# First weights loaded between the parts of the memory and used channel by channel; GpSimd adds up squares and layer-norm sums

## Chip, cores and metric

One NeuronCore of a Trainium2 chip runs the whole program; nothing is shared with another core. The metric is the device time of one execution in microseconds (us). The kernel before was timed three times. Engines are named as the profile names them: PE (TensorE matmuls), PEld (its weight loads), DVE (VectorE), ACT (ScalarE), POOL (GpSimd), SP (SyncE, which only issues DMAs).

## The reference

Two residual blocks over 256 tokens of width 1024, all in float32. Only the first block's opening and its convolution branch are touched by the change:

```python
h     = rms_norm(x, norm_g);  mem_h = rms_norm(mem, mem_norm_g)      # sums over 1024 channels
c_glu, c_gate, d_q, d_k, d_v, d_gate, x_q, x_gate, merge = split(h @ w_in)
k, v  = split(mem_h @ w_mem_kv)                                      # memory's keys and values
u     = conv31(a * sigmoid(b)) + dw_b                                # depthwise, causal, a, b = split(c_glu)
u     = layer_norm(u, ln_g, ln_b)                                    # needs sum(u) and sum(u*u) over channels
y_conv = (silu(u) * silu(c_gate)) @ w_conv_proj
y     = g0 * y_conv + g1 * y_diff + g2 * y_mem;  x = x + y @ w_out
```

The second block (stick-breaking attention, a recurrence, and a retrieval of 128 of 16384 single-neuron experts for each token) follows and ends the program.

## The kernel before

Activations lie transposed: 128 partitions, 8 chunks of channels, 256 tokens. Weights of the first block and of the second block's projections come as 94 blocks of 1 MB (`STREAM`, in the order of use), each as two halves `raw` of 128x1024 elements, issued by SP. A float32 product is made of three fast ones: `prep` (line 234) has ACT round a half to `whi` (line 247) and DVE subtract to get the rest, `wlo` (line 248); an activation is split in the same way into a high and a low part. A block is then 48 matmuls of 128x256, three for each of 16 pairs of chunk and column (`linT`, line 292, for transposed results, `linN`, line 330, for results with tokens on the partitions). `raw` has 5 buffers, `whi` and `wlo` 4 each, so that a cast waits until PE has used the half that lies four halves back. Matmuls against `ONES` (the statistics, named `stat` or `att`) are in full float32.

Start of the program (lines 475 to 505): the memory `m_t` is loaded in four pieces of two chunks, then the two halves of the first weights, then `x` in two pieces, constants, and then the stream. ACT and DVE multiply the memory by its gain and split it (`gain_col`, line 410: `mgh`, `mgl`); ACT squares it and PE sums the squares over partitions and chunks in eight `ONES` matmuls (`rms_sq`, line 435); `rstd_of` makes the reciprocal root on ACT and DVE, `tok_scalar` turns it to tokens on partitions (PE, line 420). The first four blocks, `linN`, multiply the memory; the scale is applied when ACT evicts the result to `vm` (line 503). Beside them `x` is normalised (`rms_cols`, lines 428 and 405: for each chunk DVE makes `nrm`, ACT casts it to `hh`, DVE subtracts to `hl`); block 5 is the first that needs `hh` and `hl`.

The convolution (lines 523 to 549) is 248 operations `tap` on DVE, 128x256 each, 62 for each pair of chunks. They go into a list `bg` and are taken from it in portions (`BG`, by an estimated cost) after each block; `background(.., True)` pins them behind the last `wlo`. They run beside all of the branches up to line 689. Then lines 693 to 699 make the two sums of the layer norm: ACT squares `cacc`, and PE adds `cacc` and the squares over partitions and chunks, 16 `ONES` matmuls. Each is issued as soon as its data is there in the scheduler's own reckoning, so they are spread over the last 60 us of the taps. Lines 700 to 717 make the normalised `cn`, lines 719 to 720 gate it.

A scheduler places every instruction on its engine's queue when the program is built; on the chip each queue runs strictly in that order. POOL does almost nothing until the second block's retrieval, at 600 us.

## Time and profile before

| | |
|---|---|
| three runs | 1292.05, 1288.19, 1291.80 us; median 1291.8 us |
| the profiled execution | 1291.35 us, of which the span of instructions 1289.6 us |
| PE busy | 1253.5 us (97%) |
| DVE busy | 937.0 us (73%) |
| ACT busy | 457.3 us (35%) |
| POOL busy | 214.6 us (17%), 1.5 us of it before 620 us |
| DMA | 340.76 MB, mean 264 GB/s |
| chain that ended last | PE 43%, issue 20%, DMA 16%, DVE 11%, POOL 6%, ACT 3% |

Busy time of PE is modelled from overlapping matmuls, so a full row does not say that PE ran at its peak; the distance between the starts of two matmuls says more. Waits are read from the profile's list of who waited for whom, order and distances from the timeline, and the chain shows what ended last. The granted clock of PE was at its upper level (2.4 GHz) in all of the first 600 us.

### The profile page before, as it was taken

Reading aid. Unit: us, or ns where it says so; the run is one execution under the profiler, and the core shown is the slowest. Engines: PE = TensorE matmul, PEld = TensorE weight load, DVE = VectorE, ACT = ScalarE, POOL = GpSimd, SP = SyncE. Lnnn points to the kernel's source line nnn. Section 1 sums busy time; section 2 is a strip of 40 time slices with the busy share of each in tenths; the row PEclk is TensorE's granted clock in tenths of the full one; section 3 lists DMA queues with packets and bytes.
Section 4 is the critical chain, followed back from the end, with each engine's and each line's share of the span. In section 5 each row is a group of like instructions: output and inputs, shape, how many; then the busy total and the mean of one; then the engine's idle time right before and its main releaser. Section 6 shows DMA issues by size and latency. Waiting matters only on the chain.

```text
span 1289.6 us, 24478 instructions
## 1 busy us (share of the span) xinstructions
PE 1253.5 (97%) x9948; PEld 1211.0 (94%) x9948; DVE 937.0 (73%) x1806; ACT 457.3 (35%) x741; POOL 214.6 (17%) x222
## 2 busy tenths in 40 slices
PE   8999999999999999998999899999999999999995
PEld 7999999989999999977999899999999999999884
DVE  6889988888998777855899864588545886445444
ACT  7545677578646556955431100010000000000001
POOL 0000000000000000000013443222342225333331
PEclk9999999999999999999999999999999999999998
DMA  8655443434565664423577999999999999999996
GB/s 294 189 194 182 164 138 124 132 116 147 164 200 161 196 202 157 148 67 99 181 235 240 354 409 409 409 408 363 382 383 342 356 360 392 409 409 408 409 409 231
DMA packets 94865, 340.76 MB, mean 264 GB/s; under 512 B 10576, under 2 KB 12048, under 8 KB 94624
## 3 DMA queue, kind: packets, MB, share of 16 engines
q1 hardware_dynamic: 66752, 237.98, 52.0%
q0 software_dynamic: 28000, 101.22, 20.4%
q8 instruction: 78, 1.28, 0.4%
q14 instruction: 35, 0.29, 0.1%
HBM read 338.01 MB, written 1.05 MB: 263 GB/s over the span
## 4 chain that ended last, share of the span: by engine, by line
PE 43%; issue 20%; DMA 16%; DVE 11%; POOL 6%; ACT 3%; POOLq 0%; SPq 0%; DVEq 0%; ACTq 0%
DMA gat<-in_vrow,gi 10%; PE lin L308 10%; PE lin L307 10%; PE lin L309 10%; POOL gat L1186 6%; DMA gat<-in_urow,gi 5%; DVE acc L1211 2%; PE lin L341 1%; DVE gat L1193 1%; PE lin L343 1%; PE lin L342 1%; DVE wlo L248 1%; PE stat L459 1%; ACT whi L247 1%; DVE I L983 1%
## 5 line engine op out<-in xcount | busy, mean ns | idle before, releaser
L1177 PE MATMUL y<-ga,w 128*128 128x160 f32 x2048 | 293.0, 302 | 5.6 <-DMA w<-in_v 2.8
L1177 PEld LDWEIGHTS y<-ga,w 128*128 128x128 f32 x2048 | 279.9, 190 | 13.3 <-DMA w<-in_v 10.4
L288 PE MATMUL lin<-h3f,w 128*128 128x160 f32 x2048 | 290.5, 302 | 1.7 <-ACT ga L1166 1.7
L288 PEld LDWEIGHTS lin<-h3f,w 128*128 128x128 f32 x2048 | 281.5, 191 | 2.3 <-ACT ga L1166 1.9
L248 DVE TENSOR_TENSOR wlo<-raw,whi 128x1024 fp32r<-128x1024 f32 x188 | 229.1, 1221 | 64.2 <-ACT whi L247 63.5
L247 ACT CAST whi<-raw 128x1024 fp32r<-128x1024 f32 x188 | 196.2, 1049 | 167.2 <-PE lin L308 123.8
L308 PE MATMUL lin<-hl,whi 128*128 128x256 f32 x704 | 200.2, 284 | 0.0
L309 PE MATMUL lin<-hh,wlo 128*128 128x256 f32 x704 | 199.8, 284 | 0.0
L307 PE MATMUL lin<-hh,whi 128*128 128x256 f32 x704 | 199.8, 284 | 0.0
L1211 DVE SCALAR_TENSOR_TENSOR acc<-gat,cG,acc 128x1024 f32<-128x1024 f32 x94 | 120.7, 1284 | 95.3 <-DMA gat<-in_vrow,gi 49.2
L1193 DVE CUSTOM_DVE_ANT_0 gat<-gat,hrow 128x1024 f32<-128x1024 f32 x96 | 116.6, 1224 | 29.8 <-DMA gat<-in_urow,gi 16.2
L1186 POOL DMA_INDIRECT gat<-in_urow,gi x96 | 103.4, 1077 | 198.9 <-DVE sG L1193 188.9
L309 PEld LDWEIGHTS lin<-hh,wlo 128*128 128x128 f32 x704 | 132.6, 188 | 2.2 <-issue 1.9
L308 PEld LDWEIGHTS lin<-hl,whi 128*128 128x128 f32 x704 | 132.6, 188 | 1.7 <-issue 1.4
L307 PEld LDWEIGHTS lin<-hh,whi 128*128 128x128 f32 x704 | 132.5, 188 | 1.4 <-issue 1.0
L1186 POOL DMA_INDIRECT gat<-in_vrow,gi x96 | 93.3, 972 | 162.6 <-DVE acc L1211 127.4
L1166 ACT ACTIVATE ga<-lin 128x320 f32<-128x320 f32 x64 | 27.9, 437 | 249.8 <-PE lin L288 216.7
L535 DVE SCALAR_TENSOR_TENSOR cacc<-ub,VT,cacc 128x256 f32<-128x256 f32 x240 | 103.7, 478 | 0.0
L955 POOL DMA_DIRECT2D fold<-in_con x1 | 0.7, 703 | 596.9 <-DVE gate L924 596.9
L1292 ACT COPY ga<-y 128x160 f32<-128x160 f32 x4 | 1.2, 292 | 236.2 <-PE y L1177 236.2
L1155 DVE SCALAR_TENSOR_TENSOR ga<-gp,ga 128x256 f32<-128x256 f32 (+1 forms) x60 | 29.1, 510 | 74.6 <-PE gp L1144 55.3
L308 PE MATMUL lin<-h3lo,whi 128*128 128x256 f32 x128 | 37.3, 291 | 2.3 <-DVE h3lo L384 2.3
(373 smaller groups left out, 2099.9 us busy)
## 6 DMA issues: line engine op xcount, KB each, us to landing
raw<-in_wcat SPq DMA_DIRECT2D x188, 512.0 KB
w<-in_u SPq DMA_DIRECT2D x128, 512.0 KB
w<-in_v SPq DMA_DIRECT2D x128, 512.0 KB
gat<-in_urow,gi POOLq DMA_INDIRECT x96
gat<-in_vrow,gi POOLq DMA_INDIRECT x96
m_t<-in_memT SPq DMA_DIRECT2D x4, 256.0 KB
xr<-in_xT SPq DMA_DIRECT2D x2, 512.0 KB
kT<-in_keysT SPq DMA_DIRECT2D x1, 1024.0 KB
```

Of the source, the lines that this page charges most:

```text
L247: nc.scalar.copy(h, raw)
L248: state["sub"] = nc.vector.tensor_sub(l, raw, h.bitcast(F32))
L288: nc.tensor.matmul(ps[:, a], ws[a][:, c * P:(c + 1) * P], x[:, c], start=c == 0, stop=c == 7)
L307: nc.tensor.matmul(ps[:, a], wh, ah[:, c], start=(a, c) in first, stop=False)
L308: nc.tensor.matmul(ps[:, a], wh, al[:, c], start=False, stop=False)
L309: nc.tensor.matmul(ps[:, a], wl, ah[:, c], start=False, stop=(a, c) in last)
L535: nc.vector.scalar_tensor_tensor(cacc[:, c], s, w, cacc[:, c], op0=ALU.mult, op1=ALU.add)
L1155: state["dve"] = nc.vector.scalar_tensor_tensor(g_[:, :, tl], p_, 1.0 / GSCALE, g_[:, :, tl], op0=ALU.mult, op1=ALU.mult)
L1177: nc.tensor.matmul(yT[c // 2][:, c % 2, :D], ws[a][:, c * P:(c + 1) * P], g[:, a], start=False, stop=i == 63 and (a, c % 2) == (1, 1))
L1186: nc.gpsimd.indirect_dma_start(g, None, src, bass.IndirectOffsetOnAxis(gi[:, 0, k:k + 1].bitcast(U32), 0))
L1193: nc.vector.tensor_tensor_reduce(out=g, in0=g, in1=h, scale=1.0, scalar=0.0, op0=ALU.mult, op1=ALU.add, accum_out=sG[:, k:k + 1])
L1211: state["sum"] = nc.vector.scalar_tensor_tensor(acc[m], g, cG[:, k:k + 1], acc[m], op0=ALU.mult, op1=ALU.add)
```

## The change

1. The first weights come between the pieces of the memory: `m_t` piece 1, the vectors, half 1 of block 1, pieces 2 and 3, half 2, piece 4. The halves of block 2 are issued before `x` and the constants.
2. Gains and weight splits are written in the order in which those loads come, and block 1 (`linN(.., True)`) goes channel by channel, both token halves of a chunk one after the other, so that it can begin with the first chunks. The third product of each triple is now the one with `wlo`.
3. The memory's squares are made by POOL (four `tensor_mul` of 128x512); POOL adds the last three up (two `tensor_add`). PE sums two matmuls' worth ahead of block 1 and two behind it, four in place of eight.
4. The layer norm's sums: after each pair of chunks ACT squares `cacc`, and POOL (for the first three pairs) or DVE (for the last) adds it to a running sum: `rx` for the values, `sums[0]` for the squares. PE then needs 3 `ONES` matmuls in place of 16.
5. Four small operations for the second block's recurrence (`la`) are held back until the last merge gate.

```diff
-        def prep(i):
+        def load(i, a):
+            raw = spool.tile([P, 1024], F32, name="raw", bufs=5)
+            nc.sync.dma_start(raw, srcs[i][:, a * 1024:(a + 1) * 1024])
+            return raw
+
+        def prep(i, raws=None, between=None):
...
-                raw = spool.tile([P, 1024], F32, name="raw", bufs=5)
-                nc.sync.dma_start(raw, srcs[i][:, a * 1024:(a + 1) * 1024])
+                raw = load(i, a) if raws is None else raws[a]
+                if between is not None:
+                    between(a)
...
-        def linN(act):
+        def linN(act, channelwise=False):
...
+            if channelwise:
+                seq = [(t, c) for c in range(8) for t in range(2)]
+                first, last = seq[:1], seq[-1:]
+            else:
+                seq = [(t, c) for t in range(2) for c in range(8)]
+                first, last = [(0, 0), (1, 0)], [(0, 7), (1, 7)]
...
+                nc.tensor.matmul(ps[:, t], xh, wh, start=(t, c) in first, stop=False)
+                nc.tensor.matmul(ps[:, t], xl, wh, start=False, stop=False)
+                nc.tensor.matmul(ps[:, t], xh, wl, start=False, stop=(t, c) in last)
...
-            nc.sync.dma_start(m_t[:, 0:2], memT[:, 0:2])
+            def m_load(k):
+                nc.sync.dma_start(m_t[:, 2 * k:2 * k + 2], memT[:, 2 * k:2 * k + 2])
+
+            m_load(0)
             nc.sync.dma_start(VT, vec)
-            for k in range(1, 4):
-                nc.sync.dma_start(m_t[:, 2 * k:2 * k + 2], memT[:, 2 * k:2 * k + 2])
-            prep(0)
+            raws = [load(0, 0)]
+            m_load(1)
+            m_load(2)
+            raws.append(load(0, 1))
+            m_load(3)
+            raws1 = [load(1, a) for a in range(2)]
...
+            m_gains(0)
+            prep(0, raws, lambda a: [gain_col(m_t, "mem_norm_g", mgh, mgl, c) for c in (2, 3, 4, 5)] if a else None)
+            for c in (6, 7):
+                gain_col(m_t, "mem_norm_g", mgh, mgl, c)
+
+            stm = statp()
+            msq = [smt("sqs", 512, 1), smt("sq"), smt("sq")]
+            for k in range(4):
+                q = msq[min(k, 2)] if k < 3 else smt("gate", 512, 3)
+                nc.gpsimd.tensor_mul(q.rearrange("p (a b) -> p a b", a=2), m_t[:, 2 * k:2 * k + 2],
+                                     m_t[:, 2 * k:2 * k + 2])
+                if k > 1:
+                    nc.gpsimd.tensor_add(msq[1], msq[1], q)
+                if k == 0:
+                    for b in range(2):
+                        nc.tensor.matmul(stm[:, :T], ONES, q[:, b * T:(b + 1) * T], start=b == 0, stop=False)
+            rm = smt("rm", T, 1)
+            prep(1, raws1)
...
             for j in range(4):
-                ps = linN((mgh, mgl))
+                ps = linN((mgh, mgl), j == 0)
+                if j == 0:
+                    for b in range(2):
+                        nc.tensor.matmul(stm[:, :T], ONES, msq[1][:, b * T:(b + 1) * T], start=False, stop=b == 1)
+                    rstd_of(stm[:, :T], 1.0 / 1024, T, out=rm)
+                    rmt = tok_scalar(rm, "rmt")
...
+            def conv_sums(j):
+
+                def f():
+                    e = nc.gpsimd if j < 3 else nc.vector
+                    x = cacc[:, 2 * j:2 * j + 2]
+                    sq = smt("sq" if j else "sqs", 512, 2 if j else 1)
+                    nc.scalar.square(sq.rearrange("p (a b) -> p a b", a=2), x)
+                    if j == 0:
+                        sums.append(sq)
+                        e.tensor_add(rx, x[:, 0], x[:, 1])
+                    else:
+                        for k in range(2):
+                            e.tensor_add(rx, rx, x[:, k])
+                        e.tensor_add(sums[0], sums[0], sq)
+                return f
...
+                bg.append((0.0, conv_sums(j)))
                 background(BG[0], True)
...
-            for c in range(0, NC, 2):
-                sq = smt("sq")
-                nc.scalar.square(sq.rearrange("p (a b) -> p a b", a=2), cacc[:, c:c + 2])
-                for k in range(2):
-                    nc.tensor.matmul(s1[:, :T], ONES, cacc[:, c + k], start=c + k == 0, stop=c + k == 7)
-                    nc.tensor.matmul(s2[:, :T], ONES, sq[:, k * T:(k + 1) * T], start=c + k == 0, stop=c + k == 7)
+            nc.tensor.matmul(s1[:, :T], ONES, rx, start=True, stop=True)
+            for k in range(2):
+                nc.tensor.matmul(s2[:, :T], ONES, sums[0][:, k * T:(k + 1) * T], start=k == 0, stop=k == 1)
...
-            nc.scalar.activation(la, lam, AF.Abs)
+            with tc.issue_after(state["gate"].ins):
+                nc.scalar.activation(la, lam, AF.Abs)
```

What the change moves on the queues is shown at three places. The numbers ahead of the rows are places in an engine's queue; lines in the changed kernel are its own.

PE between block 1 and block 2 of the changed kernel (L352 to L354 are `linN`'s three products; before, L341 to L343 with all eight `stat` matmuls in the first rows of the queue), and POOL from the start:

```order
47 L352 MATMUL lin<-whi,mgh 128x256
48 L353 MATMUL lin<-whi,mgl 128x256
49 L354 MATMUL lin<-wlo,mgh 128x256
50 L537 MATMUL stat<-sq,ONES 128x256 x2
51 L352 MATMUL lin<-whi,mgh 128x256
```

```order
6 L520 ISA
7 L520 TENSOR_TENSOR sqs<-m_t 128x512
8 L520 TENSOR_TENSOR sq<-m_t 128x512 x2
9 L523 TENSOR_TENSOR sq<-sq 128x512
10 L520 TENSOR_TENSOR gate<-m_t 128x512
11 L523 TENSOR_TENSOR sq<-sq,gate 128x512
12 L587 TENSOR_TENSOR rx<-cacc 128x256
13 L590 TENSOR_TENSOR rx<-rx,cacc 128x256 x2
14 L591 TENSOR_TENSOR sqs<-sqs,sq 128x512
```

Block 2 stands on PE behind the two matmuls of L537, and these wait for POOL's sixth operation (row 11). The two of the first squares (L526) are the head of the queue. ACT where `x` is normalised, before and then with the change (`hh` is line 384 before and 395 now, the cast of weights 247 and 253, the eviction `vm` 503 and 541):

```order
31 L247 CAST whi<-raw 128x1024
32 L384 CAST hh<-nrm 128x256 x2
33 L247 CAST whi<-raw 128x1024
34 L384 CAST hh<-nrm 128x256 x2
35 L503 ACTIVATE vm<-lin,rmt 128x256 x2
36 L247 CAST whi<-raw 128x1024
37 L384 CAST hh<-nrm 128x256 x2
38 L247 CAST whi<-raw 128x1024
39 L384 CAST hh<-nrm 128x256 x2
```

```order
25 L395 CAST hh<-nrm 128x256 x2
26 L253 CAST whi<-raw 128x1024
27 L395 CAST hh<-nrm 128x256
28 L253 CAST whi<-raw 128x1024
29 L541 ACTIVATE vm<-lin,rmt 128x256 x2
30 L557 ACTIVATE le<-stat 128x2
31 L395 CAST hh<-nrm 128x256 x5
```

Five of the eight casts now stand behind the twelfth weight cast (row 28) and the eviction of block 4. The third place is PE in the layer norm's sums: before, ten of the 16 matmuls in one piece, and now all three that are left, 482 linear matmuls later:

```order
2461 L308 MATMUL lin<-hl,whi 128x256
2462 L698 MATMUL stat<-cacc,ONES 128x256
2463 L699 MATMUL att<-sq,ONES 128x256
2464 L698 MATMUL stat<-cacc,ONES 128x256
2465 L699 MATMUL att<-sq,ONES 128x256
2466 L698 MATMUL stat<-cacc,ONES 128x256
```

```order
2939 L314 MATMUL lin<-hl,whi 128x256
2940 L751 MATMUL stat<-rx,ONES 128x256
2941 L315 MATMUL lin<-hh,wlo 128x256
2942 L313 MATMUL lin<-hh,whi 128x256
2943 L314 MATMUL lin<-hl,whi 128x256
2944 L753 MATMUL att<-sqs,ONES 128x256 x2
```

The last four of the 16 stood up to linear matmul 2812 of the program; the three now stand at 2855 to 2858.

## Rows read from the trace of the kernel before

**Rows 1.** Time by stage: busy us of each engine, granted clock, DMA share, GB/s.
```profile
core 0: us, PE busy (x) PEld busy (x) DVE busy (x) ACT busy (x) POOL busy (x), PEclk, DMA share, GB/s
...
11.00:21.00 10.00, 10.00 (x71) 9.44 (x70) 7.94 (x12) 8.21 (x15) 0.00 (x0) 1.00 1.01 397
...
250.00:420.00 170.00, 169.26 (x1366) 163.38 (x1365) 149.64 (x268) 113.77 (x182) 0.00 (x0) 1.00 0.50 157
```

**Rows 2.** Chain that ended last, in order of time: start us, us, what.
```profile
401.13 0.43 PE stat L698 x2
402.15 0.86 PE att L699 x4
```

**Rows 3.** Timeline of the start, all engines, PE's rows: start us, us, what.
```profile
18.50 0.28 PE L341 MATMUL lin<-whi,mgh 128*128 128x256 f32 x1
...
18.62 0.28 PE L342 MATMUL lin<-wlo,mgh 128*128 128x256 f32 x1
...
18.95 0.60 PE L420 MATMUL stat<-ONES,rm 1*128 1x1 f32 x4
```

**Rows 4.** Chain that ended last: block 5 begins.
```profile
37.98 0.22 PE lin L307
```

**Rows 5.** Timeline of ACT at the start: memory's fourth piece, second weight cast, casts of x.
```profile
8.36 0.91 ACT L412 ACTIVATE mgh<-m_t,VT 128x256 fp32r<-128x256 f32 x2 [0.49 <-DMA m_t<-in_memT]
...
11.26 1.03 ACT L247 CAST whi<-raw 128x1024 fp32r<-128x1024 f32 x1
...
37.46 0.71 ACT L384 CAST hh<-nrm 128x256 fp32r<-128x256 f32 x2
```

**Rows 6.** Timeline of DVE at the start: splits of memory, weights and x.
```profile
7.50 0.88 DVE L413 SCALAR_TENSOR_TENSOR mgl<-m_t,VT,mgh 128x256 fp32r<-128x256 f32 x2 [0.53 <-ACT mgh L412]
...
10.85 1.23 DVE L248 TENSOR_TENSOR wlo<-raw,whi 128x1024 fp32r<-128x1024 f32 x1 [0.50 <-ACT whi L247]
...
38.74 0.75 DVE L384 TENSOR_TENSOR hl<-nrm,hh 128x256 fp32r<-128x256 f32 x2
```

**Rows 7.** Timeline of POOL in the second block: products of 128x256.
```profile
626.87 1.53 POOL L998 TENSOR_TENSOR cs<-V 128x256 f32<-128x256 f32 x1 [25.58 <-DVE V L988]
636.47 0.62 POOL L998 TENSOR_TENSOR cs<-V 128x256 f32<-128x256 f32 x1 [8.08 <-DVE V L988]
...
719.09 0.62 POOL L998 TENSOR_TENSOR cs<-V 128x256 f32<-128x256 f32 x1 [1.56 <-DVE V L988]
```

**Rows 8.** Timeline of DVE around 627 us.
```profile
626.70 1.22 DVE L248 TENSOR_TENSOR wlo<-raw,whi 128x1024 fp32r<-128x1024 f32 x1
...
628.43 0.43 DVE L982 MAX8 BS<-cs 128x8 f32<-128x256 f32 x1 [0.24 <-POOL cs L998]
```

**Rows 9.** Timeline of DVE around 719 us.
```profile
719.25 1.53 DVE L1193 CUSTOM_DVE_ANT_0 gat<-gat,hrow 128x1024 f32<-128x1024 f32 x1
```

**Rows 10.** The page's costliest groups: count | busy us, mean ns of one | idle before.
```profile
L1193 DVE CUSTOM_DVE_ANT_0 gat<-gat,hrow 128x1024 f32<-128x1024 f32 x96 | 116.6, 1224 | 29.8 <-DMA gat<-in_urow,gi 16.2
```

**Rows 11.** Timeline of PE: first and last of ten statistics matmuls before the layer norm.
```profile
344.30 0.59 PE L698 MATMUL stat<-cacc,ONES 128*128 128x256 f32 x2
...
348.43 0.47 PE L309 MATMUL lin<-hh,wlo 128*128 128x256 f32 x1
```

**Rows 12.** Ten-microsecond windows before the layer norm (columns as in rows 1).
```profile
350.00:360.00 10.00, 10.00 (x88) 10.00 (x87) 9.80 (x19) 5.22 (x6) 0.00 (x0) 1.00 0.46 144
...
400.00:410.00 10.00, 10.00 (x82) 9.84 (x81) 6.25 (x12) 6.64 (x10) 0.00 (x0) 1.00 0.48 157
```

**Rows 13.** Timeline of DVE: last tap and the layer norm's mean.
```profile
397.32 0.48 DVE L535 SCALAR_TENSOR_TENSOR cacc<-ub,VT,cacc 128x256 f32<-128x256 f32 x1
...
401.60 0.42 DVE L701 TENSOR_SCALAR rm<-stat 128x256 f32<-128x256 f32 x1 [1.38 <-PE stat L698]
```

**Rows 14.** Timeline of ACT around the layer norm: squares or weight casts, their waits.
```profile
391.40 1.05 ACT L247 CAST whi<-raw 128x1024 fp32r<-128x1024 f32 x1 [1.76 <-PE lin L308]
...
392.97 1.28 ACT L354 ACT_TABLE_LOAD   x1
```

More of the change, by code (lines that the diff above doesn't have):

```diff
@@ L334, in linN @@
             ps = lin_ps[0].tile([P, 2, T], F32, name="lin")
-            for t in range(2):
-                for c in range(8):
-                    wh = hs[c // 4].rearrange("p (c j) -> p c j", c=4)[:, c % 4]
-                    wl = ls[c // 4].rearrange("p (c j) -> p c j", c=4)[:, c % 4]
-                    xh = ah[:, c, t * P:(t + 1) * P]
-                    xl = al[:, c, t * P:(t + 1) * P]
-                    nc.tensor.matmul(ps[:, t], xh, wh, start=c == 0, stop=False)
-                    nc.tensor.matmul(ps[:, t], xh, wl, start=False, stop=False)
-                    nc.tensor.matmul(ps[:, t], xl, wh, start=False, stop=c == 7)
+            if channelwise:
[4 more added lines that the diff above has]
+                first, last = [(0, 0), (1, 0)], [(0, 7), (1, 7)]
+            for t, c in seq:
+                wh = hs[c // 4].rearrange("p (c j) -> p c j", c=4)[:, c % 4]
+                wl = ls[c // 4].rearrange("p (c j) -> p c j", c=4)[:, c % 4]
+                xh = ah[:, c, t * P:(t + 1) * P]
+                xl = al[:, c, t * P:(t + 1) * P]
+                nc.tensor.matmul(ps[:, t], xh, wh, start=(t, c) in first, stop=False)
+                nc.tensor.matmul(ps[:, t], xl, wh, start=False, stop=False)
+                nc.tensor.matmul(ps[:, t], xh, wl, start=False, stop=(t, c) in last)
             ahead()
@@ L479, in build, with m_gains @@
             m_t = bigt("m_t")
-            nc.sync.dma_start(m_t[:, 0:2], memT[:, 0:2])
+            def m_load(k):
+                nc.sync.dma_start(m_t[:, 2 * k:2 * k + 2], memT[:, 2 * k:2 * k + 2])
+            m_load(0)
             nc.sync.dma_start(VT, vec)
-            for k in range(1, 4):
-                nc.sync.dma_start(m_t[:, 2 * k:2 * k + 2], memT[:, 2 * k:2 * k + 2])
-            prep(0)
+            raws = [load(0, 0)]
[4 more added lines that the diff above has]
+            raws1 = [load(1, a) for a in range(2)]
             for k in range(2):
                 nc.sync.dma_start(x_t[:, 4 * k:4 * k + 4], xT[:, 4 * k:4 * k + 4])
+            mgh, mgl = bigt("mgh", F32R), bigt("mgl", F32R)
+            def m_gains(a):
+                for c in range(4 * a, 4 * a + 2):
+                    gain_col(m_t, "mem_norm_g", mgh, mgl, c)
+            m_gains(0)
+            prep(0, raws, lambda a: [gain_col(m_t, "mem_norm_g", mgh, mgl, c) for c in (2, 3, 4, 5)] if a else None)
+            for c in (6, 7):
+                gain_col(m_t, "mem_norm_g", mgh, mgl, c)
+            stm = statp()
[11 more added lines that the diff above has]
+            prep(1, raws1)
             nc.sync.dma_start(CT, con)
             nc.sync.dma_start(ident, con0[:, :P])
-            mgh, mgl = bigt("mgh", F32R), bigt("mgl", F32R)
-            for c in range(NC):
-                gain_col(m_t, "mem_norm_g", mgh, mgl, c)
-            rm = smt("rm", T, 1)
-            stm = statp()
-            for c in range(0, NC, 2):
-                rms_sq(m_t, stm, c, NC)
-            rstd_of(stm[:, :T], 1.0 / 1024, T, out=rm)
-            rmt = tok_scalar(rm, "rmt")
             vm = big.tile([P, 2, 1024], F32, name="vm", tag="big")
@@ L536, in tap @@
                 return f
+            sums = []
+            def conv_sums(j):
[12 more added lines that the diff above has]
+                return f
             for j in range(4):
@@ L693, in build @@
             s1, s2 = statp(), attp()
-            for c in range(0, NC, 2):
-                sq = smt("sq")
-                nc.scalar.square(sq.rearrange("p (a b) -> p a b", a=2), cacc[:, c:c + 2])
-                for k in range(2):
-                    nc.tensor.matmul(s1[:, :T], ONES, cacc[:, c + k], start=c + k == 0, stop=c + k == 7)
-                    nc.tensor.matmul(s2[:, :T], ONES, sq[:, k * T:(k + 1) * T], start=c + k == 0, stop=c + k == 7)
+            nc.tensor.matmul(s1[:, :T], ONES, rx, start=True, stop=True)
+            for k in range(2):
+                nc.tensor.matmul(s2[:, :T], ONES, sums[0][:, k * T:(k + 1) * T], start=k == 0, stop=k == 1)
             mu, mm, var = smt("rm", T, 1), smt("nrm", T), smt("nrm", T)
```

## The prediction

> **What bounds the kernel now.** I read the stages by time first. From 11 to 21 us PE is busy all the time and the DMA engines are full, at 397 GB/s; from 250 to 420 us PE is busy for 169.26 of 170 us, DVE for 149.64 and ACT for 113.77 [rows 1]. PE is what time is made of here, so a PE instruction that goes is worth its whole length, as long as DVE still delivers the split weights in time. The chain gives the length of the instructions in question: one full-float32 matmul of 128x256 takes 0.43 us (two take 0.86) [rows 2], while the products of a block start 0.12 us apart [rows 3], 48 x 0.12 = 5.8 us for a block. The timelines of the start then give the marks: block 1 is over and the scale's transposition begins at 18.95 us [rows 3], block 5, the first that needs `x` normalised, begins at 37.98 us [rows 4]. Between the two lie three blocks and two small groups of statistics, 19.03 us, which the change keeps in content.
>
> **The start of the program.** The change takes four of eight statistics matmuls off PE, 4 x 0.43 = 1.7 us, and lets block 1 begin with the first chunks. What it needs does not come earlier: before, the second half of the first weights was the last of 2.28 MB, and ACT cast it at 11.26 us without a wait; now the memory's fourth piece is the last of the same 2.28 MB. The memory's second piece now ends 1.23 MB, as its fourth did before, for which ACT waited until 8.36 us [rows 5]; I take 8.1 us for POOL. Were DVE left alone, the second half's `wlo` would be done at some 12.6 us, 22 products would follow it, and block 1 would end at 15.4 us; with two matmuls of statistics (0.86) block 2 would begin at 16.3 us.
>
> But DVE is not left alone. POOL's operation at 626.87 us took 1.53 us where one alone takes 0.62 [rows 7]: it was issued 0.17 us after a `wlo` on DVE that ended at 627.92, and ended 0.48 us behind that [rows 8]. The other way round, POOL's operation of 719.09 us ran to 719.71 [rows 7], and the DVE operation issued at 719.25 took 1.53 us [rows 9] against a mean of 1.224 [rows 10]. In both cases DVE had two inputs in SBUF and POOL read SBUF, and the later one stood until the earlier was through. That is what the splits `mgl` (memory and `mgh`) and `wlo` (`raw` and `whi`) are, and what POOL's six new operations are.
>
> The Trainium skill (SBUF — State Buffer, section Who interferes with whom) has it as a rule that such a pair excludes each other for the whole instruction and that the order of issue decides who waits. By that rule, with which these rows agree in both directions, the start comes out late as in the next paragraph; without it, early as in the first rival.
>
> So I add up both engines' work on one resource, from 8.1 us until block 2 can begin. POOL has five operations of 512 elements left. Their length is not in the trace: between 0.62 us (no more than for 256) and 1.24 us (twice that); I take 1.2, since the work is by element: 6.0 us. DVE has three `wlo` at 1.2 us and six `mgl` at 0.44 us [rows 6], 6.2 us. That is 12.2 us, to 20.3 us; with the fourth `wlo` slipping in, 21.5 us. I take 20.7. Whoever of the two goes first, the other's share is needed too, because block 2 stands on PE behind the two matmuls that wait for POOL's last sum. They take 0.86 us: block 2 at 21.5 us, where before the same point was at 18.95 us [rows 3]. **2.6 us late.**
>
> Then `x`. Five of its eight casts now stand on ACT behind the twelfth weight cast, which needs the last matmul of block 4. From there: that cast 1.03 us, block 4's eviction and a small one some 0.9, and five chunks one after the other on DVE, each 0.44 for `nrm` and 0.38 for `hl` [rows 5, 6], 4.1 us; 6.0 us in all. PE has 24 products of block 5 and 21 of block 6 that the scheduler put between, 45 x 0.12 = 5.4 us, and waits 0.6 to 0.7 us. Before, the last `hl` came at 39.5 us, ahead of its product. The start is thus **3.3 us late**; with POOL's operation at its lower end 0.4 us late, with no exclusion 19.03 + 16.3 + 0.7 = 36.0 instead of 37.98 us, 1.9 us early.
>
> **The layer norm's sums.** PE loses 13 of 16 matmuls, 13 x 0.43 = 5.6 us, in stages where it is never idle. ACT keeps its four squares. POOL's additions for the first three pairs lie beside other work, but hold DVE up by 2 x 0.62 + 1.2 = 2.4 us in the second and third pair, and DVE itself gets three additions for the last, 2 x 0.44 and 0.88 for 512 elements [rows 6], 1.8 us, between the last tap (397.32 us) and the mean, which stood 1.38 us waiting for PE before [rows 13]; PE comes to its three matmuls 43 products (5.2 us) later than to the last four before, so I see no wait there. Ten of the removed matmuls ran together from 344.30 to 348.43 us [rows 11], in a stretch where DVE is busy 9.80 of 10 us [rows 12]: there PE may run into a `wlo` that isn't there yet. Bounds of that loss: nothing, since DVE falls to 6.25 of 10 us from 400 us on [rows 12] and splits lie about two halves ahead, and 4.3 us, all ten. I take 1.0, nearer the first, because the lead is regained in the 50 us that follow. **4.6 us gained.**
>
> **Small things.** The program now loads activation tables four times more often, three of them around the recurrence's `la`, at 1.28 us each on ACT; the weight casts there wait 1.76 us each for PE [rows 14] and stand two halves ahead of their use, which hides it; without that cover up to 3.2 us would show. The four squares of the memory off ACT and the later arrival of `x` cost nothing: its sum now stands 71 products into the next blocks. What comes behind the layer norm is only shifted.
>
> **The sum.** The profiled execution took 1291.35 us, span 1289.6, 0.45 us under the median of 1291.8. 1291.35 + 3.3 - 4.6 = **1290.0 us**.
>
> **Rivals.** *GpSimd slips into VectorE's gaps:* if POOL's operations are shorter or VectorE is hardly held, the start gains 1.9 and the sums about 4.9: 1284.6 us. For it: DVE is busy only 7.94 of 10 us from 11 to 21 us [rows 1]. Against: the durations of [rows 7 to 9]. *GpSimd starts late (slower than before):* its first product heads PE's queue and its last holds block 2, and the trace has no first operation whose start can be seen (the one at 626.87 us came after 25.58 us of idling [rows 7]). Up to 8.1 us a late start is free; each microsecond beyond that is one for the kernel; above 5 us it makes it measurably slower. At 7.5 us: 1291.35 + 3.3 + 7.5 - 4.6 = 1297.5 us. *VectorE becomes the bound:* all ten matmuls at 344 us were filling a wait, the gain shrinks to 1.3 and the kernel takes 1291.35 + 3.3 - 1.3 = 1293.4 us.
>
> The Trainium skill (GPSIMD Engine Reference, section Instruction dispatch) says that the first call of freshly loaded code costs about 6 us more, with nothing to be seen in the profile. By that, an estimate, the first product would be through 0.5 + 6 + 1.2 = 7.7 us into the program, ahead of 8.1, and the second rival would be out; no run here shows it.
>
> **The numbers.** Chances: the forecast 0.47, the first rival 0.30, late GpSimd 0.14, VectorE as bound 0.09. The forecast's own range is 1287 to 1293 us. From 1284 to 1296 us lie the forecast, VectorE as bound, the upper two thirds of the first rival and the mildest part of the late start; about 2 in 10 stay out. A measurement of this kernel tells 0.3% from no change, 3.9 us. Faster by more: nearly all of the first rival and the lower end of the forecast, 0.35. Slower by more: the late start and the ends of the other two, 0.17. Between: 0.48.
>
> **What would show it.** Right: POOL's first six operations in the profile after last well over 1.2 us where DVE splits, or DVE's splits grow; the two matmuls behind block 1 wait for POOL to about 20 us; block 5 begins near 40.5 us; the marks behind the layer norm lie 1 to 2 us earlier than before. Wrong: block 5 near 36 us (first rival), a head of PE's queue that waits beyond 9 us (second), PE waiting for `wlo` around 330 to 400 us (third), or a difference that arises behind 600 us, where I expect none.

## The result and the profile after

The changed kernel takes 1302.2 us (median of 5 runs, 1300.33 to 1303.84) where the kernel before takes 1291.8 us (5 runs, 1288.19 to 1293.46): a ratio of 1.0084, 95% interval 1.0072 to 1.0096. It is **slower by about 10.8 us** (by the ratio), outside the range that was given (1284 to 1296) and on the other side of the forecast. The profiled execution took 1302.2 us, its span is 1300.4 us, 10.8 us over the span before.

Time by stage, from 300 us on in the kernel before and then in the changed kernel (columns as in [rows 1]):

```profile
300.00:360.00 60.00, 59.91 (x477) 58.06 (x476) 54.95 (x101) 46.52 (x69) 0.00 (x0) 1.00 0.49 154
400.00:440.00 40.00, 40.00 (x337) 39.78 (x336) 27.88 (x43) 27.90 (x39) 0.00 (x0) 1.00 0.54 175
```

```profile
11.00:21.00 10.00, 8.89 (x58) 8.58 (x58) 9.30 (x11) 4.86 (x8) 3.52 (x3) 1.00 1.03 401
...
300.00:360.00 60.00, 54.27 (x436) 52.16 (x435) 51.55 (x95) 45.60 (x68) 4.69 (x3) 1.00 0.45 142
...
400.00:440.00 40.00, 36.31 (x280) 35.94 (x280) 29.33 (x51) 25.61 (x36) 0.00 (x0) 0.91 0.50 159
```

From 11 to 21 us PE is no longer busy all the time, as it was in [rows 1], and from 300 to 360 us it idles 5.7 us. In the kernel before the same 60 us had 59.91 us of PE, and from 400 to 440 us, where 3.7 us are missing now, PE was busy without a break. The list of those that PE waited for, from 20 to 540 us (us, times, longest), has rows that have no counterpart before (there the list has one row, 0.6 us for `y`, which the changed kernel has too); its four largest:

```profile
PE lin L313 <- ACT smc L768: 3.7, 1, 3.7
PE att L701 <- ACT sig L700: 2.5, 2, 1.4
PE lin L315 <- DVE wlo L254: 1.7, 2, 1.2
PE lin L313 <- ACT sig L731: 1.5, 1, 1.5
```

These are the four places to look at: the eviction `smc` behind the conv layer norm (line 768), the copy `sig` of the transposed softmax (line 700), `wlo`, and the first merge gate (`sig`, line 731).

How far the kernel is behind can be read at any time from the start of a block's first `wlo` on DVE:

| block | before | after | late |
|---|---|---|---|
| 14 | 81.64 | 83.72 | 2.1 |
| 47 | 320.34 | 322.53 | 2.2 |
| 55 | 367.39 | 372.97 | 5.6 |
| 67 | 439.74 | 450.33 | 10.6 |
| 84 | 548.28 | 558.40 | 10.1 |

Nothing happens between blocks 14 and 47. The losses are made at the start, from 310 to 370 us and at the layer norm.

**The start.** POOL and DVE of the changed kernel up to 16 us (start us, us, what, idle before and its releaser):

```profile
4.87 1.03 POOL L520 TENSOR_TENSOR sqs<-m_t 128x512 f32<-128x512 f32 x1 [4.41 <-DMA m_t<-in_memT]
7.55 3.02 POOL L520 TENSOR_TENSOR sq<-m_t 128x512 f32<-128x512 f32 x2 [1.64 <-DMA m_t<-in_memT]
10.64 1.35 POOL L523 TENSOR_TENSOR sq<-sq 128x512 f32<-128x512 f32 x1
11.96 1.22 POOL L520 TENSOR_TENSOR gate<-m_t 128x512 f32<-128x512 f32 x1
13.25 1.35 POOL L523 TENSOR_TENSOR sq<-sq,gate 128x512 f32<-128x512 f32 x1
```

```profile
7.62 2.05 DVE L254 TENSOR_TENSOR wlo<-raw,whi 128x1024 fp32r<-128x1024 f32 x1 [0.63 <-ACT whi L253]
9.59 5.29 DVE L424 SCALAR_TENSOR_TENSOR mgl<-m_t,VT,mgh 128x256 fp32r<-128x256 f32 x4
14.80 1.21 DVE L254 TENSOR_TENSOR wlo<-raw,whi 128x1024 fp32r<-128x1024 f32 x1
```

The first `wlo` takes 2.05 us where one took 1.23 [rows 6], four `mgl` take 5.29 us, three times the 0.44 each of before, and the second `wlo` starts at 14.80, just behind POOL's last operation (13.25 + 1.35 = 14.60). The two engines take turns: the first of the two products from 7.55 us takes 1.04 us, the second, issued while `wlo` is at work, 2.02; and the four `mgl` end at 10.85, 12.27, 13.45 and 14.88 us, each 0.28 to 0.29 us behind the end of one of POOL's operations (10.56, 11.99, 13.17 and 14.60). PE in the same stage:

```profile
14.15 0.41 PE L353 MATMUL lin<-whi,mgl 128*128 128x256 f32 x1
...
14.56 0.28 PE L352 MATMUL lin<-whi,mgh 128*128 128x256 f32 x1
...
18.81 1.03 PE L537 MATMUL stat<-sq,ONES 128*128 128x256 f32 x4
19.48 0.47 PE L352 MATMUL lin<-whi,mgh 128*128 128x256 f32 x1
...
25.76 0.60 PE L431 MATMUL stat<-ONES,rm 1*128 1x1 f32 x4
...
28.90 1.02 PE L408 MATMUL stat<-sqs,ONES 128*128 128x256 f32 x4
```

Block 1 waits 1.1 us for the second `wlo` and ends at 18.81 us; the two matmuls of L537 run at once, since POOL has long been through, and block 2 begins at 19.48 us, where it began before. The transposition of the memory's scale (L431) comes only at 25.76 us now, and the sum of `x`'s squares (L408) behind it, at 28.90 us where it ran at 21.02 us before. In the first two rows a product's length falls from 0.41 to 0.28 us, and with it the distance of two from 0.21 to 0.12 us, of which more at the end.

**The layer norm.** ACT of the changed kernel:

```profile
413.52 0.51 ACT L385 ACTIVATE rv<-nrm,VT 128x256 f32<-128x256 f32 x1 [1.73 <-DVE nrm L757]
414.06 0.42 ACT L386 ACTIVATE rs<-rv 128x256 f32<-128x256 f32 x1
414.85 1.04 ACT L253 CAST whi<-raw 128x1024 fp32r<-128x1024 f32 x1 [0.37 <-PE lin L314]
415.80 0.41 ACT L387 ACTIVATE rs<-rs 128x256 f32<-128x256 f32 x1
...
416.67 1.28 ACT L768 ACT_TABLE_LOAD   x1
417.97 1.57 ACT L768 ACTIVATE smc<-lin 128x512 f32<-128x512 f32 x3
```

PE behind it, and the two windows of ten microseconds:

```profile
418.62 0.58 PE L313 MATMUL lin<-hh,whi 128*128 128x256 f32 x1 [3.69 <-ACT smc L768]
...
423.91 0.38 PE L313 MATMUL lin<-hh,whi 128*128 128x256 f32 x1
```

```profile
410.00:420.00 10.00, 6.31 (x43) 5.94 (x42) 7.39 (x16) 7.05 (x11) 0.00 (x0) 0.86 0.58 187
420.00:430.00 10.00, 10.00 (x71) 10.00 (x70) 6.30 (x12) 6.96 (x13) 0.00 (x0) 0.79 0.17 63
```

The kernel before has the same chain, with a weight cast at the same place:

```profile
404.53 0.42 ACT L375 ACTIVATE rs<-rv 128x256 f32<-128x256 f32 x1
405.28 1.05 ACT L247 CAST whi<-raw 128x1024 fp32r<-128x1024 f32 x1 [0.33 <-PE lin L308]
406.23 0.41 ACT L376 ACTIVATE rs<-rs 128x256 f32<-128x256 f32 x1
...
408.41 1.09 ACT L714 ACTIVATE smc<-lin 128x512 f32<-128x512 f32 x2
```

There PE did not need `smc` before 410.8 us, when block 60 was over. In the changed kernel PE's last sum (L753) ended at 412.15 us. ACT then made the reciprocal root (L385 to L388) with a weight cast in the middle of it, loaded a table and evicted `smc`; PE, which had 22 products left of block 60, stood 3.69 us. Behind this, 24 products stood 0.21 us apart in place of 0.12: the granted clock is 0.86 and 0.79 in the two windows, and the distances are those of the lower level, 1.2 GHz, until 424.1 us. That is 24 x 0.09 = 2.2 us more.

### The profile page after: what moved, and what is told of

Its sections match the earlier page's. It is cut to its first block, busy times and chain, and to the rows that moved or that the text cites. A ratio compares the mean times of both kernels' runs of the same rounds, so it can differ in the third digit from the quotient of the medians.

```text
span 1300.4 us, 24438 instructions
## 1 busy us (share of the span) xinstructions
PE 1251.0 (96%) x9914; PEld 1209.8 (93%) x9914; DVE 944.9 (73%) x1809; ACT 461.1 (35%) x741; POOL 229.8 (18%) x235
## 3 DMA queue, kind: packets, MB, share of 16 engines
q8 instruction: 78, 1.28, 0.4%
## 4 chain that ended last, share of the span: by engine, by line
PE 41%; issue 19%; DMA 18%; DVE 11%; POOL 5%; ACT 5%; SPq 0%; POOLq 0%; DVEq 0%; ACTq 0%
DMA gat<-in_vrow,gi 14%; PE lin L314 10%; PE lin L313 10%; PE lin L315 10%; POOL gat L1241 5%; DMA gat<-in_urow,gi 4%; DVE wlo L254 1%; DVE acc L1266 1%; ACT whi L253 1%; PE lin L354 1%; PE lin L352 1%; PE lin L353 1%; DVE gat L1248 1%; PE lin L294 1%; PE stat L470 1%
## 5 line engine op out<-in xcount | busy, mean ns | idle before, releaser
L1266 DVE SCALAR_TENSOR_TENSOR acc<-gat,cG,acc 128x1024 f32<-128x1024 f32 x94 | 120.7, 1284 | 94.8 <-DMA gat<-in_vrow,gi 94.4
L590 POOL TENSOR_TENSOR rx<-rx,cacc 128x256 f32<-128x256 f32 x4 | 6.7, 1674 | 225.2 <-DVE cacc L573 225.2
```

What stands on the lines that cost most here:

```text
L1266: state["sum"] = nc.vector.scalar_tensor_tensor(acc[m], g, cG[:, k:k + 1], acc[m], op0=ALU.mult, op1=ALU.add)
```

## The experiments

Each series has its own runs of the kernel before, so that ratios, and not medians, are compared from one series to another.

| run | edit | median us | ratio to before, 95% interval |
|---|---|---|---|
| (the change) | | 1302.2 | 1.0084 [1.0072, 1.0096] |
| e1 | start alone | 1303.04 | 1.0094 [1.0078, 1.011] |
| e2 | layer norm's sums alone | 1295.93 | 1.0044 [1.0028, 1.006] |
| e3 | change, second `smc` released | 1297.32 | 1.0056 [1.0042, 1.0071] |
| e4 | e3, order in the attention restored | 1291.18 | 1.0007 [0.9998, 1.0017] |
| e5 | change, no POOL at the start | 1300.37 | 1.0076 [1.0061, 1.0091] |
| e6 | e2, second `smc` released | 1287.95 | 0.998 [0.9968, 0.9991] |
| e7 | e4, no POOL at the start | 1291.89 | 1.001 [0.9998, 1.0023] |
| e8 | change, `la` not held back | 1297.2 | 1.0055 [1.004, 1.007] |
| e9 | e5, PSUM buffer of its own for `x`'s sum | 1299.42 | 1.0066 [1.0053, 1.0078] |
| e10 | e7, PSUM buffer of its own for `x`'s sum | 1287.47 | 0.9972 [0.9961, 0.9983] |

Places on PE are counted below in linear products from the program's start; 48 are a block.

### e1 and e2: the two halves of the change

e1 is the change without its parts 4 and 5, e2 the kernel before with part 4 alone. The edits, from the change and from the kernel before:

```diff
-                bg.append((0.0, conv_sums(j)))
...
-            nc.tensor.matmul(s1[:, :T], ONES, rx, start=True, stop=True)
...
+            for c in range(0, NC, 2):
...
+                    nc.tensor.matmul(s1[:, :T], ONES, cacc[:, c + k], start=c + k == 0, stop=c + k == 7)
...
-            with tc.issue_after(state["gate"].ins):
```

```diff
+                bg.append((0.0, conv_sums(j)))
...
-            for c in range(0, NC, 2):
...
+            nc.tensor.matmul(s1[:, :T], ONES, rx, start=True, stop=True)
```

> The kernel before with the start of the change alone (loads interleaved, block 1 channel by channel, memory's squares on GpSimd); the layer norm's sums are 16 matmuls as before and la is not held back. Theory: the start is 2.1 us late, and it is the start that moves the scheduler's order in the attention of the last heads (transposes of the last softmax one product ahead of their use instead of 18), so that PE idles some 6 us between 300 and 360 us although no sum of the conv layer norm has been touched; no wait of PE behind the layer norm's sums, which stand at linear matmul 2790, 90 products ahead of the end of block 60. 1291.8 + 2.1 + 6 = 1299.9 us. Rival: the waits between 300 and 360 us come from GpSimd's additions for the layer norm: then only the start is late, 1293.9 us, and PE waits nowhere between 300 and 360 us.

> The kernel before with the layer norm's sums of the change alone (GpSimd and VectorE add up, 3 matmuls in place of 16); start and la as before. Theory: PE saves 13 x 0.43 = 5.6 us and does not idle between 300 and 360 us, but its last sum stands at linear matmul 2879, one product ahead of the end of block 60 (2880), and ACT's eviction smc, for which block 61 waits, comes 6.3 us after the last sum: PE waits 6.2 us there and then runs 24 products at 0.21 in place of 0.12 us, 2.2 us: 1291.8 - 5.6 + 8.4 = 1294.6 us. Rival one: GpSimd's additions make the waits between 300 and 360 us, 6 us: about 1300 us. Rival two: the sums are pure gain, 1286.2 us.

Neither half alone is faster. e1, in which no sum of the layer norm is touched, has the waits of the attention stage to the tenth (PE's waits and the window):

```profile
PE att L682 <- ACT sig L681: 2.5, 2, 1.4
PE lin L313 <- ACT sig L712: 1.5, 1, 1.5
```

```profile
300.00:360.00 60.00, 56.02 (x431) 54.00 (x430) 49.78 (x94) 44.59 (x68) 0.00 (x0) 0.97 0.42 141
```

So it is **the start that makes PE wait at 320 to 340 us**, 300 us later; GpSimd does nothing there in e1, and the first rival is out. e1 is 3 us slower than the theory's 1299.9. The trace puts PE 8.8 us behind at linear product 2858, with a granted clock of 0.97 in the window above; the other 3 us arise behind 540 us, most of them behind 590 us. No experiment followed them, but the traces show a difference there: from 590 to 630 us PE is busy for 34.1 us in the change, in e1 and in e10, and for 34.6 us in the kernel before, while the granted clock is 0.96 before, 0.91 in the change and 0.87 in e1 and e10. Each is one profiled execution, so whether the kernel or the execution sets this is open.

How a start can do that is seen in PE's order. The transposes of the last softmax and the product that needs ACT's copy of them, before and with the change (numbers are places in PE's queue):

```
2324 L641 MATMUL att<-ident,pp 128x128 x2
...
2343 L644 MATMUL att<-sig,vd 128x256
```

```
2336 L698 MATMUL att<-ident,pp 128x128 x3
2337 L315 MATMUL lin<-hh,wlo 128x256
2338 L701 MATMUL att<-sig,vd 128x256
```

There were 18 products between, and there is one now. On ACT the gate of the last head pair had stood ahead of the reciprocal root's two table loads; now it stands between them and brings a third, so that the softmax ahead of the transposes is later. The scheduler writes this order from its own reckoning of the whole program, so work at 20 us moves rows at 310 us. Which of the start's edits turns it is open.

e2 has no such waits, and shows what the sums bring by themselves:

```profile
PE lin L307 <- ACT smc L730: 4.2, 1, 4.2
PE lin L309 <- DVE wlo L248: 2.2, 2, 1.7
```

```profile
300.00:360.00 60.00, 57.63 (x462) 55.50 (x462) 55.66 (x100) 45.49 (x68) 3.87 (x3) 1.00 0.46 155
...
400.00:440.00 40.00, 35.81 (x278) 35.37 (x277) 27.34 (x44) 25.11 (x37) 0.00 (x0) 0.91 0.44 150
```

The wait for `smc` was put at 6.2 us and is 4.2 us; the half pace behind it lasts for 25 products, 2.4 us in place of 2.2; and PE idles 2.4 us from 300 to 360 us, mainly for two `wlo` (2.2 us). Rival two, that the sums are pure gain, is out.

### e3 and e6: the second `smc` released

```diff
-            table(nc.scalar.activation(smc[:, 0:2], linT(h), AF.Sigmoid), LN_EXP)
+            nc.scalar.activation(smc[:, 0:2], linT(h), AF.Sigmoid)
+            table(nc.scalar.activation(smc[:, 2:4], linT(h), AF.Sigmoid), LN_EXP)
...
-            for j in range(1, 4):
+            for j in range(2, 4):
```

> The change with one edit: the second of the four sigmoid evictions smc is no longer held back behind the layer norm's reciprocal root, so that block 61 does not wait for the sums; the next such wait could come 48 products (5.8 us) later. Theory: the wait of 3.7 us at 415 us and the 24 products at half pace behind it (2.2 us) go: 1302.2 - 5.9 = 1296.3 us, with an activation table load or two more on ACT (up to 1.3 us each) as the risk. Rival: PE was waiting for the sums' chain in any case and waits one block later: 1301 to 1302 us.

> The start of before with the sums of the change, and the second sigmoid eviction no longer held back (the second run with the edit of the third). Theory: of the second run's 1295.9 us go the 4.2 us in which PE waited for smc and some 3.6 us that the half pace behind it cost (granted clock 0.91 over 40 us): 1288.1 us, 3 us under the kernel before (1291.0 us in that series). Rival: the wait turns up one block later, 1294 us or more.

Both came out within about 1 us. In e3 the wait is gone, and with it the lower clock:

```profile
400.00:440.00 40.00, 40.00 (x335) 39.84 (x334) 33.51 (x56) 29.19 (x41) 0.00 (x0) 1.00 0.57 191
```

So the loss at the layer norm is shown to be this one wait and what follows it: from linear product 2812 to 2928 the change loses 6.4 us against the kernel before (its own three sums deducted), e3 nothing. Not all of it reaches the end: the profiled execution of e3 is 5.1 us shorter than that of the change, and by the ratios of the two series the gain is 3.6 us. e6 is the change's part 4 with its wait taken away: the first version that beats the kernel before, by 2.6 us (interval 1.2 to 4.1). It is also the measure of the sums: its blocks are 0.6 us early at block 14, still only 0.7 us at block 55, though ten of the removed matmuls (4.1 us) lie ahead of that, and 3.0 us at block 67. **Of 5.6 us that PE saves, 2.5 us arrive** by then; of the rest, 2.2 us stand in the list as two waits for `wlo`. DVE is busy for 77.47 of the 80 us from 320 to 400, so it has little room to deliver them earlier; no run tested this.

### e4: the order in the attention

```diff
+                rts.append(state["rstd"][0])
...
-                i = nc.scalar.activation(g, ps, AF.Silu)
+                with ExitStack() as s:
+                    if j == 3 and lo is odl:
+                        s.enter_context(tc.issue_after(rts[2].ins))
+                    i = nc.scalar.activation(g, ps, AF.Silu)
```

> As the run before it, and the gate of the last differential head pair is held back behind the reciprocal root of the pair before: the last softmax's transposes then stand 22 products ahead of their use in place of one, and two table loads follow one another where there were three. Theory: the waits of 1.4 and 1.1 us for ACT's copy of the transposed softmax at 320 and 334 us go, and part of the 1.5 us for the first merge gate: 1296.3 - 3 = 1293.3 us. Rival: ACT is full there and the wait only moves to another product: 1296 us or more.

The gain against e3 is 6.1 us, twice what was expected. The three waits for `sig` are gone from PE's list, and the window from 300 to 360 us, of e3 and then of e4, reads:

```profile
300.00:360.00 60.00, 54.55 (x436) 52.42 (x435) 51.60 (x95) 46.04 (x68) 4.68 (x3) 1.00 0.42 142
```

```profile
300.00:360.00 60.00, 58.60 (x473) 56.49 (x472) 55.89 (x99) 46.90 (x69) 3.26 (x3) 1.00 0.45 155
```

4.05 us of busy PE come back in this stage. By PE's marks it is the whole loss: from linear product 1500 to 2300 the change and e3 fall 4.7 us behind the kernel before, and e4 stays level with it. The profiled execution of e4 reached block 14 1.1 us later than that of e3 (granted clock 0.69 from 14.5 to 20 us) and gained 3.9 us on it behind 590 us, where the granted clock is 0.91 in e3 and 0.96 in e4 (590 to 630 us); so the rest of the 6.1 us is not shown to come from the order.

### e8: `la`

```diff
-            with tc.issue_after(state["gate"].ins):
-                nc.scalar.activation(la, lam, AF.Abs)
+            nc.scalar.activation(la, lam, AF.Abs)
```

> The change without its fifth part: la is not held back, three activation tables fewer are loaded. Both the theory and the prediction put no price on la: 1302 us. Rival: its table loads hold up weight casts, up to 3.2 us: 1299 us.

The rival's side: without the fifth part the change costs 7.1 us and not 10.8. But its mechanism isn't the one that the rival named. ACT and PE of e8 at the layer norm:

```profile
413.58 0.51 ACT L385 ACTIVATE rv<-nrm,VT 128x256 f32<-128x256 f32 x1 [0.35 <-DVE nrm L757]
414.13 0.42 ACT L386 ACTIVATE rs<-rv 128x256 f32<-128x256 f32 x1
414.58 0.42 ACT L387 ACTIVATE rs<-rs 128x256 f32<-128x256 f32 x1
...
416.76 1.09 ACT L768 ACTIVATE smc<-lin 128x512 f32<-128x512 f32 x2
```

```profile
417.41 0.39 PE L313 MATMUL lin<-hh,whi 128*128 128x256 f32 x1 [1.47 <-ACT smc L768]
```

The last sum ended at 412.92 us, 0.8 us later than in the change, and `smc` is 1.2 us earlier: the chain between them takes 3.8 us in place of 5.8. Of these 2.0 us, 1.3 lie on ACT, where no weight cast stands between L386 and L387, and 0.7 on DVE ahead of it, where a `wlo` no longer stands in the chain. PE waits 1.47 us in place of 3.69, and runs on at 0.12 us; from product 2812 to 2928 e8 loses 1.7 us where the change loses 6.4 (1.2 us of this gain are lost in its attention stage, at a granted clock of 0.97 from 300 to 360 us). The kernel before, which does not hold `la` back either, has the cast and the `wlo` in its chain (5.6 us long), so it was not the hold that put them there: without it the scheduler finds, with the moved sums, an order that leaves them out. The table loads around `la` (386 to 390 us) hide, as forecast.

### e5, e7, e9 and e10: the start

e5 takes POOL out of the start, e7 does the same to e4:

```diff
-                nc.gpsimd.tensor_mul(q.rearrange("p (a b) -> p a b", a=2), m_t[:, 2 * k:2 * k + 2],
-                                     m_t[:, 2 * k:2 * k + 2])
+                nc.scalar.square(q.rearrange("p (a b) -> p a b", a=2), m_t[:, 2 * k:2 * k + 2])
                 if k > 1:
-                    nc.gpsimd.tensor_add(msq[1], msq[1], q)
+                    nc.vector.tensor_add(msq[1], msq[1], q)
```

> The change with the memory's four squares on ACT and their two additions on VectorE, so that GpSimd does nothing at the start; all orders behind the first blocks are those of the change. Theory: GpSimd's operations and VectorE's splits exclude each other; without GpSimd the first wlo takes 1.2 in place of 2.1 us, the four mgl behind it 1.8 in place of 5.3, the second wlo is done by some 12.3 in place of 16.0 us, and block 2 begins near 17.4 in place of 19.5 us: 1302.2 - 2.1 = 1300.1 us. Rival: ACT's casts, which now stand behind the squares, or the loads set the start in any case: block 2 near 19.5 us, 1302 us.

> The change with all three edits: squares on ACT and VectorE at the start, the gate of the last head pair held back, the second sigmoid eviction released. Theory: the fourth run's 1291.2 us less the 2.1 us of the start: 1289.1 us. Rival: the start's gain is lost again where x is normalised (five casts behind block 4's eviction): 1291 us.

DVE of e5, and PE where block 2 begins:

```profile
7.55 1.23 DVE L254 TENSOR_TENSOR wlo<-raw,whi 128x1024 fp32r<-128x1024 f32 x1 [1.53 <-ACT whi L253]
8.69 1.67 DVE L424 SCALAR_TENSOR_TENSOR mgl<-m_t,VT,mgh 128x256 fp32r<-128x256 f32 x4
...
11.14 1.23 DVE L254 TENSOR_TENSOR wlo<-raw,whi 128x1024 fp32r<-128x1024 f32 x1 [0.17 <-ACT whi L253]
```

```profile
17.54 0.47 PE L352 MATMUL lin<-whi,mgh 128*128 128x256 f32 x1
```

The operations that took 2.05 and 5.29 us in the change take 1.23 and 1.67 us, and block 2 begins at 17.54 us (17.4 was expected): **it was POOL that held DVE.** Yet block 14 is 1.9 us late, as in the change (2.1), and e7 is no faster than e4. That e5's time came out as expected (1300.4 for 1300.1 us) is thus in part luck; its gain over the change, 1.0 us by the ratios, is within the intervals. The lead is lost where `x` is normalised: PE waits for `hl` in six pieces from 37.9 to 44.1 us, some 3 us in sum. `x`'s squares are summed by PE at 29.97 us, though DVE had them at 19.7 us; their PSUM tile is `stat`, which has one buffer, and this holds the memory's scale until its transposition has been copied. e9 and e10 give `x` another buffer:

```diff
-        def sq_sum(x, n):
+        def sq_sum(x, n, pool=None):
...
-            ps = statp()
+            ps = statp() if pool is None else pool()
...
-                    rms_cols(x_t, "norm_g", hh, hl)
+                    rms_cols(x_t, "norm_g", hh, hl, r=rms_r(x_t, ps=sq_sum(x_t, NC, attp)))
```

> The run without GpSimd at the start (e5) with one more edit: x's sum of squares goes into a PSUM buffer of its own (att) and no longer shares the single buffer stat with the memory's sums and their transposition. Theory: in the change x's sums cannot start before the memory's scale has left that buffer (26.5 us in the change, 27.8 us in e5), so x is normalised late and block 5 waits for hl in pieces, which took back the whole lead of e5's block 2 (17.5 us). With a buffer of its own x's sums stand at linear product 87, near 22.3 us in place of 30 us; the waits for hl, some 3 us in sum, go, and the weights of block 14 come 1 to 1.5 us earlier than in the kernel before where e5 had them 1.9 us later: 3 us off e5, some 1297.5 us beside a kernel before of 1291. Rival: the late order of casts and evictions on ACT sets x in any case: no change against e5, 1300.5 us.

> All three edits of e7 and the second PSUM buffer for x's sums. Theory: e7 (0.6 to 1.3 us over the kernel before) less the 3 us of the start: some 1289 us beside a kernel before of 1291. Rival: no change against e7, 1292 us.

PE of e9:

```profile
21.83 1.02 PE L408 MATMUL att<-sqs,ONES 128*128 128x256 f32 x4
```

The sum is 8 us earlier, the waits for `hl` are gone, and block 14 starts at 79.93 us, 3.6 us ahead of e5 and 1.7 us ahead of the kernel before. The mechanism is shown; of the 3 us that were expected in the time of the whole kernel, e9 has 1.3 (by the ratios, within the intervals), e10 against e7 4.9 (clear of them). In the profiled executions e9 is still 5.0 us ahead of e5 at block 94 and 2.0 us at the end. From there to the end the twelve profiled executions of this document take between 639.7 and 644.3 us, and what sets this was not followed. e10 is the fastest of all kernels here: 0.9972 of before, 3.6 us less. Its two windows beside those of the change:

```profile
300.00:360.00 60.00, 58.68 (x473) 56.55 (x472) 56.29 (x99) 44.98 (x62) 3.70 (x3) 1.00 0.51 158
...
400.00:440.00 40.00, 40.00 (x334) 39.83 (x333) 31.12 (x49) 28.86 (x41) 0.00 (x0) 1.00 0.54 176
```

That it is faster than e6 (0.998) is not shown; their intervals overlap. At block 84 e10 is 4.3 us ahead of the kernel before and its span is 1.8 us less; 3.8 us are lost between blocks 84 and 94, the stretch in which the granted clock was lower (0.87 against 0.96 from 590 to 630 us), and 1.4 us come back behind it.

## Why the prediction was wrong

The sum of the prediction and what the trace of the changed kernel has in its place (us):

| term | predicted | found |
|---|---|---|
| start | +3.3 | +2.1 |
| 13 matmuls fewer on PE | -5.6 | -5.6 |
| lost again behind the removed matmuls (waits for `wlo`) | +1.0 | +2.8 |
| order in the last attention heads | none | +4.7 |
| layer norm: `smc` and the lower clock | none | +6.4 |
| behind the layer norm | none | +0.4 |
| sum | -1.3 | +10.8 |

The found ones come from PE's own marks, the start of the same linear product in both kernels:

| behind linear product | before | after | late |
|---|---|---|---|
| 1500 | 210.91 | 212.98 | 2.1 |
| 2300 | 335.75 | 342.54 | 6.8 |
| 2812 | 402.66 | 405.40 | 2.7 |
| 2928 | 416.46 | 426.86 | 10.4 |

At product 2812 the kernel before has all of its 16 matmuls behind it (6.9 us) and the change none of its three (1.3 us). So the order in the attention is 6.8 - 2.1 = 4.7; what was lost again behind the removed matmuls is 2.7 + 6.9 - 6.8 = 2.8, of which 1.7 us stand in the list as waits for `wlo`; and the layer norm is 10.4 - 2.7 - 1.3 = 6.4: the wait of 3.69 us, 2.2 us at the lower clock, and the first products behind the wait.

- **The step that failed first** is "PE comes to its three matmuls 43 products (5.2 us) later than to the last four before, so I see no wait there". It looked at the wait ahead of the sums. The wait was behind them, and cost 6.4 us where the forecast had none: before, 68 products were left after the last sum up to the end of block 60, 8 us, and the chain from there to `smc` took 5.6 us; with the change 22 were left, 2.6 us, and the chain took 5.8 us. Both numbers stood in the order and in the trace of before. e3 and e6 show it by taking the dependence away.
- **The second** is a term that the sum does not have. The forecast speaks of the order at three places and takes all other rows to cost what they cost before; at 310 us, between them, the moved rows cost 4.7 us. e1 shows that the start alone makes the waits there, e4 that the order is their cause. "What comes behind the layer norm is only shifted" held to 0.4 us in the profiled execution.
- **The third** is "Small things", which puts no price on the held-back `la`. The cover of its table loads held (the 3.2 us named there without it have no working; three loads of 1.28 us are 3.84). But e8 puts the fifth part at 3.7 us by the ratios, and at 3.4 us in the trace (6.73 in place of 10.12 us late at block 84): with the hold, the weight cast and the `wlo` stay in the layer norm's chain, as they were in the kernel before, and without it they are out.
- **The start** was right in its mechanism and wrong in its sum. The forecast added up all the work of both engines, to 20.7 us, and let block 2 wait for POOL's last sum, to 21.5 us. POOL was done at 14.60 us. The two took turns, so that of DVE's work only one `wlo` and four `mgl` lay ahead of POOL's end; and a product of POOL's alone took 1.03 us, where 1.2 was taken. DVE's second `wlo`, done at 16.0 us, then set block 1's end, and block 2 was on time at 19.48 us. The 2.1 us come from the transposition (0.7 us, now behind block 2's beginning) and from `x` (1.3 us in block 5: two products 0.78 us apart where PE waits for `hl` ahead of 41.8 us, and smaller gaps). The forecast had 0.7 us for `x` and blamed the casts behind block 4's eviction; e9 shows the single PSUM buffer instead. The first rival, with block 1 over at 15.4 us, was too early as well: without POOL (e5) it ended at 16.87 us, for PE had no wait in it behind 9.2 us and ran its products 0.21 us apart until 14.4 us. Block 5 of the changed kernel began at 38.66 us, between the sign for the forecast (40.5) and that for the first rival (36).
- **The sums** were right in kind: a loss between nothing and 4.3 us was allowed for, 1.0 was taken, 2.8 was found, and PE did wait for `wlo` where the third sign of being wrong had it (330 to 400 us). The rival with VectorE as the bound was a little nearer (4.3) than the value taken, but with 0.09 it had little weight, and it gives 1293.4 us.
- **The rivals.** GpSimd did not start late: its first operation ran at 4.87 us, as soon as its data was there, and took 1.03 us; in the profiles of e1, e3, e4 and e8 it ran at 3.96 to 4.06 us, 1.03 us long. The Trainium skill (GPSIMD Engine Reference, section Instruction dispatch) has some 6 us more for the first call of freshly loaded code, from which the prediction estimated that this product would be through at 7.7 us; it was through at 5.0 to 5.9 us. Nothing of the 6 us is seen here; whether this code counts as freshly loaded, no run shows. GpSimd did not slip into DVE's gaps either. The rival on the slower side had a slow start of POOL as its mechanism; none had a wait behind a moved instruction.

The Trainium skill (SBUF — State Buffer, section Who interferes with whom) has the exclusion of the two engines for the length of an instruction. The durations above agree: 2.05 and 5.29 us with POOL at work, 1.23 and 1.67 us without, and each `mgl` ends within 0.29 us of the end of a POOL operation.

## What to carry to other kernels

When a change makes an instruction later, ask what stands behind it up to the next buffer that must come free, and count the work that PE has until then: here 22 products were left of 68, and the chain needed 50. When a scheduler writes the order, an edit at one end of the program moves rows at the other; compare the order of all engines over the whole program, and look first at the places where one engine is a single product ahead of another. A tile with a single buffer joins two chains that have no data in common.

## What the runs showed of the hardware

- POOL's product of 128x512 took 1.03 us alone and up to 2.02 us beside DVE, its sum 1.35 us beside DVE; DVE's splits took up to three times as long beside it (5.29 us for four, 1.67 without), so POOL's 6.9 us of additions and products cost DVE 4.4 us in these five operations.
- Behind a wait of 3.69 us PE ran 24 products 0.21 us apart, at a granted clock of 0.86 and 0.79; behind 1.47 us (e8) it ran on at 0.12 us. The length alone doesn't decide it: from 300 to 360 us, behind the same three waits (1.4, 1.1 and 1.5 us), the granted clock is 1.00 in the change and 0.97 in e1.
- At the start, products of block 1 stood 0.21 us apart until 14.4 us although the row of the granted clock says 1.00 from 11 to 21 us; the trace has no record of the granted clock ahead of 14.5 us, and the column says 1.00 where there is none. So it is in the kernel before: four passes of its statistics matmuls take 2.08 us at 9.84 us, and four of L537 in the change 1.03 us at 18.81 us. The sentence ahead of the prediction that the clock was at its upper level in all of the first 600 us does not hold for the first 12.8 us. The distance between two products says more of the pace than that column.
- From 590 to 630 us PE was busy for nearly the same time in these seven profiles (34.1 to 34.6 us), at a granted clock of 0.96 (before, e4), 0.91 (the change, e3) or 0.87 (e1, e7, e10).
